# Token factors of the input norm moved behind the projections in a hybrid mLSTM and DeltaNet block, and x loaded in column slabs

## The chip, the cores and the metric

The kernel runs on one core of a Trainium2 chip. The metric is device time in microseconds (us), the median of three runs. A profile of one further execution is read beside it. Engines are named as the profile names them: PE is the matrix engine (PEld its weight loads), DVE the vector engine, ACT the scalar engine, POOL the GpSimd engine, SP the engine that only issues DMAs here. A "q" behind a name (SPq, ACTq) is the engine's sequencer, which issues DMAs.

## The reference

One decoder layer on x of 512 tokens by 2048 channels, all in float32. Cut to what matters here:

```python
def _rmsnorm(x, w=None):
    y = xf * lax.rsqrt(jnp.mean(xf * xf, axis=-1, keepdims=True) + NORM_EPS)
    return y if w is None else y * w.astype(jnp.float32)

u = _rmsnorm(h, norm_w)
proj = jnp.matmul(u, w_in.astype(jnp.float32))
(ml_q, ml_k, ml_v, ml_o, ml_z, ml_i, ml_f,
 dn_qkv, dn_z, dn_b, dn_a, gate_a, gate_b) = jnp.split(proj, idx, axis=-1)
h_a = _mlstm_chunkwise(q, k, v, i_pre, logf)               # 8 heads
h_a = _merge_heads(_rmsnorm(h_a)) * ml_norm_w * sigmoid(ml_o) * silu(ml_z)
qkv = _causal_conv_silu(dn_qkv, dn_conv_w)                 # along the tokens, width 4
h_b = _gated_delta_chunkwise(l2norm(dq), l2norm(dk), dv, beta, g)   # 16 heads
h_b = _merge_heads(_rmsnorm(h_b, dn_norm_w)) * silu(dn_z)
y = sigmoid(gate_a) * (h_a @ w_out[:2048]) + sigmoid(gate_b) * (h_b @ w_out[2048:])
return _rmsnorm(x + y, final_norm_w)
```

In the first line each token t has one factor, rsqrt(mean(x[t]^2) + eps). It multiplies the whole row of u, so it also multiplies every row of the projections, and it can be applied to them instead.

## The kernel before

Every matrix product is done in three passes with a high and a low part of each operand (`uh`, `ul` for u, `wh`, `wl` for weights). ACT makes the high part (a rounding copy, L140 for weights, L314 for u), DVE the low part (the difference, L143 and L315). PE's order is written out by hand, by the order of the code; the orders of the other engines are made by a scheduler from priorities (`urgent`, `behind`). Small pieces of work are generators that `tick()` advances, one tick per six matmuls.

The program has these stages:

- **Start.** SP issues x in eight pieces of 128 tokens by 1024 channels (L270), then the norm weights (L106) and the first four weight tiles `wr` (L172). For each of four groups of 128 tokens ACT squares and sums one half (L297), DVE the other (L299), DVE and POOL make the token factor `rs` (L301 to L304), and DVE and ACT scale the two halves of x in place (L290, L292). Then `make_u(kt)` turns one 128-channel block on PE (four transposes, L313) and ACT and DVE write `uh` and `ul` with the norm weight as a scale (L314, L315).
- **First projection**, `proj_cm(ML_Q)` with `first_block`: for each pair of channel blocks, PE transposes the blocks two ahead and then runs 12 matmuls (L257 to L259), so that u is made while it is used.
- **Three more projections, then `seven_stage`**: projections in blocks of 2 x 512 columns. Its ends are the functions `sink_z`, `sink_s`, `sink_q` and `sink_flat`, which bring the results out of PSUM through ACT and DVE.
- **Mixers** (from about 1110 to 1860 us): eight units of two DeltaNet heads, each with three projections (key, value, query), and eight mLSTM heads beside them. A projection leaves PSUM through `conv_in` (ACT's copy into `yp`, L828) and `conv_silu` (ACT's first tap, L835, and three multiply-adds of DVE, L837); `silu_end` adds the SiLU (ACT L843 into the tile `th`, DVE L844). `dn_back` inverts 128x128 triangles by blocks: among its steps DVE writes a small tile `s` (L1051), which PE needs at L1057.
- **Output projection** and final norm.

DMAs that SP and ACT issue tell of their landing by one of eight semaphores, given out in turn over both engines together (`DMAHW0` to `DMAHW7` in the listings below). A DMA that gets a semaphore for the second time waits until the DMA before it on that semaphore has landed, and the engine that issues it waits with it.

Of the kernel before, what the change touches and what calls it, by code (L numbers as in the profile page):

```python
# [8 lines left out]
F32 = mybir.dt.float32  # L9
# [6 lines left out]
P = 128  # L16
# [42 lines left out]
def hybrid_body(  # L59
# [24 lines left out]
    rows_d = dr.tile([32, S], F32, tag="rows", name="rows_d")  # L84
# [17 lines left out]
    bia = cp.tile([P, 96], F32, tag="bia", name="bia")  # L102

    def load_norms(tp, psp):
        nr = tp.tile([16, P], F32, tag="prow", name="nrow")
        nc.sync.dma_start(nr, norm_w.rearrange("(a p) -> a p", p=P))  # L106
# [20 lines left out]
    def turn_taps(crs, nr, psp):  # L127
        pt = psp.tile([P, 256], F32, tag="wk", name="pprt")
# [46 lines left out]
    def split_next():  # L175
        raw, nk, n = raws[len(parts)]
        with tc.high_priority(offset=2 * PRIO if len(parts) > SAHEAD else 0):
            hi = wp.tile([P, nk, n], F32R, tag="wh", name="wh", bufs=NSPL)
            lo = wp.tile([P, nk, n], F32R, tag="wl", name="wl", bufs=NSPL)
            with ExitStack() as first:  # L180
                if not parts:
                    first.enter_context(behind("V"))
                    first.enter_context(behind("A"))
                elif len(parts) == 1:
                    first.enter_context(tc.issue_after(done["V"]))
                    first.enter_context(tc.issue_after(done["A"]))
# [79 lines left out]
    xts = []  # L266
    for c in range(NC):
        xt = p0.tile([P, D], F32, tag=f"x{c}", name=f"xt{c}")
        for i in range(2):
            nc.sync.dma_start(xt[:, i * HD:(i + 1) * HD], x[c * P:(c + 1) * P, i * HD:(i + 1) * HD])  # L270
# [10 lines left out]
    rs = p0.tile([P, NC], F32, tag="rs", name="rs")  # L281
# [4 lines left out]
    sq, done = {}, {}  # L286

    def scale_x(c):
        with tc.issue_after(sq["V"]):
            newest["V"] = V.tensor_scalar(out=xts[c][:, 0:HD], in0=xts[c][:, 0:HD], scalar1=rs[:, c:c + 1], scalar2=None,  # L290
                                        op0=ALU.mult).ins
        newest["A"] = A.mul(xts[c][:, HD:D], xts[c][:, HD:D], rs[:, c:c + 1]).ins  # L292

    for c in range(NC):
        xt = xts[c]
        jk = p0.tile([P, HD], F32, tag="jk", name="jk", bufs=2)
        A.activation(jk, xt[:, 0:HD], AF.Square, accum_out=ss[:, c, 0:1])  # L297
        jv = p0.tile([P, HD], F32, tag="jv", name="jv", bufs=2)
        sq["V"] = V.scalar_tensor_tensor(out=jv, in0=xt[:, HD:D], scalar=1.0, in1=xt[:, HD:D], op0=ALU.mult, op1=ALU.mult,  # L299
# [5 lines left out]
        if c:  # L305
            scale_x(c - 1)
# [1478 lines left out]
```

## Time and profile before

| | us |
|---|---|
| median of 3 runs (2144.21 to 2146.49) | 2144.33 |
| profiled execution | 2143.23 |
| its span in the trace | 2141.5 |
| busy: PE / DVE / ACT / POOL | 2113.5 / 1708.0 / 1057.6 / 451.1 |

The span runs from the first to the last instruction of the trace; the execution's own time is 1.7 us longer. Busy times are sums over instructions. Matmuls overlap in the array, so a PE that is busy all the time can still differ in pace; the starts of its rows tell that.

### The profile page before, as it was taken

The page shows a single profiled execution, that of the slowest core. Times are in us where ns is not written, and L with a number is a line of the kernel's source. Part 1 is how long each engine was busy: PE and PEld are TensorE (multiplying, and loading weights), DVE is VectorE, ACT ScalarE, POOL GpSimd, SP SyncE. Part 2 cuts the span into 40 slices and gives each one's busy share as a digit, 9 for nine tenths or more (in the row PEclk, how much of TensorE's full clock was granted, in tenths as well). Part 3 has the DMA queues.
Part 4 walks back from the last instruction along what each step waited for, and adds up shares of the span by engine and source line. Part 5 has one row for each costly group of instructions (what it writes and reads, how often), then busy time and mean ns, then how long its engine had stood idle before and what let it go on. Part 6 is the DMA issues. An engine that isn't in the chain of part 4 may idle for free.

```text
span 2141.5 us, 32018 instructions
## 1 busy us (share of the span) xinstructions
PE 2113.5 (99%) x10544; PEld 1752.6 (82%) x10544; DVE 1708.0 (80%) x2981; ACT 1057.6 (49%) x2066; POOL 451.1 (21%) x667
## 2 busy tenths in 40 slices
PE   6999999999999999999999999999999999999998
PEld 5888888888888888888888888888888888887886
DVE  5888888788788778777766887888878878569887
ACT  5444454445444444444445546456465464345345
POOL 0000000000004000000003335344343363233211
PEclk9999999999999999999999999999999999999999
DMA  5355676667677767766766867777686677778895
GB/s 162 119 192 190 212 217 198 220 199 224 206 234 237 245 196 226 240 209 212 253 205 165 208 166 180 183 180 192 182 211 173 171 189 224 196 223 287 245 302 225
DMA packets 447144, 444.21 MB, mean 207 GB/s; under 512 B 197121, under 2 KB 303842, under 8 KB 446850
## 3 DMA queue, kind: packets, MB, share of 16 engines
q1 hardware_dynamic: 377618, 337.22, 53.9%
q0 software_dynamic: 24752, 72.90, 10.9%
q10 hardware_dynamic: 44608, 32.06, 4.8%
q8 instruction: 82, 1.34, 0.3%
q14 instruction: 84, 0.69, 0.1%
HBM read 348.66 MB, written 97.58 MB: 208 GB/s over the span
## 4 chain that ended last, share of the span: by engine, by line
PE 95%; DVE 2%; DMA 2%; issue 1%; SPq 0%; POOL 0%; ACT 0%; DVEq 0%; POOLq 0%; ACTq 0%
PE ps L578 18%; PE ps L580 18%; PE ps L579 18%; PE pj L257 10%; PE pj L259 9%; PE pj L258 9%; PE py L1407 2%; PE py L1409 2%; PE py L1408 2%; PE pk L915 1%; DMA wr<-in_w_out_dram 1%; PE pqk L990 1%; PE pw L1087 1%; PE pnum L1213 1%; PE po L1102 1%
## 5 line engine op out<-in xcount | busy, mean ns | idle before, releaser
L143 DVE TENSOR_TENSOR wl<-wr,wh 128x512 fp32r<-128x512 f32 (+1 forms) x522 | 444.3, 852 | 176.5 <-ACT wh L140 172.3
L140 ACT CAST wh<-wr 128x512 fp32r<-128x512 f32 (+1 forms) x522 | 373.9, 717 | 422.1 <-PE pj L258 218.5
L257 PE MATMUL pj<-uh,wh 128*128 128x512 f32 x896 | 375.8, 419 | 0.0
L259 PE MATMUL pj<-uh,wl 128*128 128x512 f32 x896 | 351.5, 392 | 0.0
L258 PE MATMUL pj<-ul,wh 128*128 128x512 f32 x896 | 349.8, 390 | 0.0
L578 PE MATMUL ps<-wh,uh 128*128 128x512 f32 x752 | 292.7, 389 | 0.8 <-DVE X L632 0.8
L579 PE MATMUL ps<-wl,uh 128*128 128x512 f32 x752 | 292.6, 389 | 0.0
L580 PE MATMUL ps<-wh,ul 128*128 128x512 f32 x752 | 292.6, 389 | 0.0
L140 ACT CAST wh<-t 128x1024 fp32r<-128x1024 f32 x120 | 126.3, 1053 | 301.7 <-PE ps L580 197.5
L533 POOL DMA_DIRECT2D t_d<-ts x104 | 56.6, 544 | 921.8 <-DVE ts L520 853.5
L579 PE MATMUL ps<-wl,suh 128*128 128x512 f32 x624 | 242.9, 389 | 0.0
L580 PE MATMUL ps<-wh,sul 128*128 128x512 f32 x624 | 242.8, 389 | 0.0
L578 PE MATMUL ps<-wh,suh 128*128 128x512 f32 x624 | 242.8, 389 | 0.0
L140 ACT CAST wh<-ts 128x512 fp32r<-128x512 f32 x240 | 147.9, 616 | 184.7 <-DVE ts L538 157.6
L143 DVE TENSOR_TENSOR wl<-t,wh 128x1024 fp32r<-128x1024 f32 x120 | 147.0, 1225 | 81.9 <-ACT wh L140 81.5
L259 PEld LDWEIGHTS pj<-uh,wl 128*128 128x128 f32 x896 | 168.3, 188 | 37.0
L257 PEld LDWEIGHTS pj<-uh,wh 128*128 128x128 f32 x896 | 169.2, 189 | 29.7
L258 PEld LDWEIGHTS pj<-ul,wh 128*128 128x128 f32 x896 | 169.3, 189 | 28.5
L143 DVE TENSOR_TENSOR wl<-ts,wh 128x512 fp32r<-128x512 f32 x240 | 164.9, 687 | 32.6 <-ACT wh L140 31.2
L578 PEld LDWEIGHTS ps<-wh,uh 128*128 128x128 f32 x752 | 141.2, 188 | 30.4 <-DVE X L632 1.2
L579 PEld LDWEIGHTS ps<-wl,uh 128*128 128x128 f32 x752 | 141.2, 188 | 29.5
L580 PEld LDWEIGHTS ps<-wh,ul 128*128 128x128 f32 x752 | 141.2, 188 | 29.2
(345 smaller groups left out, 3804.2 us busy)
## 6 DMA issues: line engine op xcount, KB each, us to landing
wr<-in_w_in_dram SPq DMA_DIRECT2D x744, 256.0 KB, 3.6
wr<-in_w_out_dram SPq DMA_DIRECT2D x138, 256.0 KB, 4.8
t_d<-ts POOLq DMA_DIRECT2D x104, 256.0 KB, 3.6
wr<-t_d SPq DMA_DIRECT2D x104, 256.0 KB, 3.7
xt<-in_x_dram SPq DMA_DIRECT2D x8, 512.0 KB, 7.2
tg_d<-X ACTq DMA_DIRECT2D x16, 256.0 KB, 4.8
tg_d<-to ACTq DMA_DIRECT2D x16, 256.0 KB, 4.6
v<-v_d SPq DMA_DIRECT2D x8, 512.0 KB, 5.6
```

The costliest lines, as they stand in the source:

```text
L140: newest["A"] = A.copy(hi, src).ins
L143: newest["V"] = V.tensor_tensor(out=lo, in0=src, in1=hi.bitcast(F32), op=ALU.subtract).ins
L257: T.matmul(ps[j], hi[:, k, wsl], uh[:, kt, :], start=(kt == 0), stop=False)
L258: T.matmul(ps[j], hi[:, k, wsl], ul[:, kt, :], start=False, stop=False)
L259: T.matmul(ps[j], lo[:, k, wsl], uh[:, kt, :], start=False, stop=(kt == KT - 1))
L533: queue.dma_start(t2_d[b % 2, i], ts[:, 0, :])
L578: T.matmul(ps[t], ah, hi, start=(g == "A" and i == 0), stop=False, skip_group_check=True)
L579: T.matmul(ps[t], ah, lo, start=False, stop=False, skip_group_check=True)
L580: T.matmul(ps[t], al, hi, start=False, stop=(i == KH - 1), skip_group_check=True)
L1407: T.matmul(ps[c], uh[:, kt, tsl], hi, start=(kt == ks[0]), stop=False)
L1408: T.matmul(ps[c], uh[:, kt, tsl], lo, start=False, stop=False)
L1409: T.matmul(ps[c], ul[:, kt, tsl], hi, start=False, stop=(kt == ks[-1]))
```

## The change

`rs` is no longer applied to x. The tiles of x go straight to the transposes, and they are loaded in column slabs: 256 channels of all tokens, 256 more, then three slabs of 512. Token groups 0 and 2 are issued by SP, 1 and 3 by ACT. The norm weights go through POOL's queue. The squares are taken during the first projection (`square_x`, one half group for each block from block 3 on), and `token_factors` makes `rs`, `rsh` (half of it) and `rsq` (with 1/sqrt(128)).

The factors come back in these places: in the scales of ACT's instructions in the sinks; in one multiplication of the gates; in the mLSTM heads' scores, weights and outputs and in the norms of the heads; and for the DeltaNet projections, which have tokens along the free axis, as a row `rsrow` broadcast to all partitions: `conv_in` becomes a multiplication on DVE. `th` in `silu_end` has one buffer in place of two.

```diff
     def load_norms(tp, psp):
-        nc.sync.dma_start(nr, norm_w.rearrange("(a p) -> a p", p=P))
+        nc.gpsimd.dma_start(nr, norm_w.rearrange("(a p) -> a p", p=P))
...
-    for c in range(NC):
-        xt = p0.tile([P, D], F32, tag=f"x{c}", name=f"xt{c}")
-        for i in range(2):
-            nc.sync.dma_start(xt[:, i * HD:(i + 1) * HD], x[c * P:(c + 1) * P, i * HD:(i + 1) * HD])
-        xts.append(xt)
-    for _ in range(2):
-        load_raw()
     load_norms(p0, psw)
+    xts = [p0.tile([P, D], F32, tag=f"x{c}", name=f"xt{c}") for c in range(NC)]
+
+    def load_x(a, b):
+        for c in range(NC):
+            (nc.scalar if c % 2 else nc.sync).dma_start(xts[c][:, a:b], x[c * P:(c + 1) * P, a:b])
+
+    load_x(0, NB)
+    load_raw()
+    load_x(NB, 2 * NB)
+    load_raw()
+    for a in range(2 * NB, D, NO):
+        load_x(a, a + NO)
...
-    def scale_x(c):
-        with tc.issue_after(sq["V"]):
-            newest["V"] = V.tensor_scalar(out=xts[c][:, 0:HD], in0=xts[c][:, 0:HD], scalar1=rs[:, c:c + 1], scalar2=None,
-                                        op0=ALU.mult).ins
-        newest["A"] = A.mul(xts[c][:, HD:D], xts[c][:, HD:D], rs[:, c:c + 1]).ins
...
+    def square_x(c, i):
+        xt, at = xts[c][:, i * HD:(i + 1) * HD], ss[:, c, i:i + 1]
+        jk = p0.tile([P, HD], F32, tag="jk", name="jk", bufs=2)
+        with tc.issue_after(done["V" if i else "A"]):
+            if i:
+                V.scalar_tensor_tensor(out=jk, in0=xt, scalar=1.0, in1=xt, op0=ALU.mult, op1=ALU.mult, accum_out=at)
+            else:
+                A.activation(jk, xt, AF.Square, accum_out=at)
+
+    def token_factors():
+        V.tensor_tensor(out=rs, in0=ss[:, :, 0], in1=ss[:, :, 1], op=ALU.add)
+        V.tensor_scalar(out=rs, in0=rs, scalar1=1.0 / D, scalar2=EPS, op0=ALU.mult, op1=ALU.add)
+        G.tensor_tensor(out=rs, in0=rs, in1=mhalf, op=ALU.pow)
+        V.tensor_scalar(out=rsh, in0=rs, scalar1=0.5, scalar2=None, op0=ALU.mult)
+        V.tensor_scalar(out=rsq, in0=rs, scalar1=float(P) ** -0.5, scalar2=None, op0=ALU.mult)
...
+        if 3 <= kt < 3 + 2 * NC:
+            square_x((kt - 3) // 2, (kt - 3) % 2)
+        if kt == 3 + 2 * NC:
+            token_factors()
...
                 with urgent(3):
-                    A.activation(o, ps, func, scale=scale)
+                    A.activation(o, ps, func, scale=scale[:, c:c + 1])
...
     def conv_in(ps, level=1):
...
         with urgent(level):
-            A.copy(yp[:, 3:S + 3], ps)
+            V.tensor_tensor(out=yp[:, 3:S + 3], in0=ps, in1=rsrow, op=ALU.mult)
...
-        th = wkb.tile([P, S], F32, tag="th", name="th", bufs=2)
+        th = wkb.tile([P, S], F32, tag="th", name="th", bufs=1)
...
         G.tensor_tensor(out=rsd, in0=ssq, in1=mhalf, op=ALU.pow)
+        G.tensor_tensor(out=rsd, in0=rsd, in1=rs, op=ALU.mult)
...
         with urgent():
-            V.tensor_tensor(out=w, in0=psc, in1=w, op=ALU.mult)
+            if first:
+                for c in range(NC):
+                    V.scalar_tensor_tensor(out=w[:, c, :], in0=psc[:, c, :], scalar=rs[:, c:c + 1], in1=w[:, c, :],
+                                           op0=ALU.mult, op1=ALU.mult)
+            else:
+                V.tensor_tensor(out=w, in0=psc, in1=w, op=ALU.mult)
```

PE's order of instructions is the same in both kernels, apart from one more small transpose and the turning of the parameters two blocks later. The other engines' orders move in three places that matter below.

The first place is ACT's start. The rows are ACT's first instructions in order, with the semaphores that each waits for (`DMAHW` the landings of DMAs, named after the engine otherwise). Before, ACT loads its table of functions at once and then squares x as it lands:

```order
L297 ACT_TABLE_LOAD
L297 ACTIVATE jk,ss<-xt_108 128x1024 [waits DMAHW0_49]
L297 ACTIVATE jk,ss<-xt_111 128x1024 [waits DMAHW2_49]
L292 ACTIVATE xt_108<-xt_108,rs 128x1024 [waits DMAHW1_49,Pool_49]
L297 ACTIVATE jk,ss<-xt_114 128x1024 [waits DMAHW4_49,Activation_49]
```

In the changed kernel the same engine stands so (`xt_114` and `xt_116` are token groups 1 and 3):

```order
L272 DMA xt_114<-in_x_dram 128x256
L272 DMA xt_116<-in_x_dram 128x256
L272 DMA xt_114<-in_x_dram 128x256
L272 DMA xt_116<-in_x_dram 128x256
L272 DMA xt_114<-in_x_dram 128x512 [waits DMAHW0_49]
L272 DMA xt_116<-in_x_dram 128x512 [waits DMAHW2_49]
L272 DMA xt_114<-in_x_dram 128x512 [waits DMAHW4_49]
L272 DMA xt_116<-in_x_dram 128x512 [waits DMAHW6_49]
L272 DMA xt_114<-in_x_dram 128x512 [waits DMAHW0_49]
L272 DMA xt_116<-in_x_dram 128x512 [waits DMAHW2_49]
L314 ACT_TABLE_LOAD [waits DVE_49]
L314 ACTIVATE uh<-put,normc 128x512 [waits PE_49] x2
```

Ten DMAs have moved ahead of ACT's table load and of its first work on u, and the last six of them wait for landings: `DMAHW0` and `DMAHW2` are waited for twice, the second time for the third slab.

The second place is the start of SP's order, before (`xt_108` to `xt_117` are the four token groups, two DMAs each):

```order
L270 DMA xt_108<-in_x_dram 128x1024 x2
L270 DMA xt_111<-in_x_dram 128x1024 x2
L270 DMA xt_114<-in_x_dram 128x1024 x2
L270 DMA xt_117<-in_x_dram 128x1024 x2
L106 DMA nrow<-in_norm_w_dram 16x128 [waits DMAHW0_49]
L172 DMA wr<-in_w_in_dram 128x2x256 [waits DMAHW1_49]
```

and in the changed kernel (`xt_113` and `xt_115` are token groups 0 and 2):

```order
L272 DMA xt_113<-in_x_dram 128x256
L272 DMA xt_115<-in_x_dram 128x256
L272 DMA xt_113<-in_x_dram 128x256
L176 DMA wr<-in_w_in_dram 128x2x256
L272 DMA xt_115<-in_x_dram 128x256 [waits DMAHW1_49]
L272 DMA xt_113<-in_x_dram 128x512 [waits DMAHW3_49]
L176 DMA wr<-in_w_in_dram 128x2x256 [waits DMAHW5_49]
L272 DMA xt_115<-in_x_dram 128x512 [waits DMAHW7_49]
```

The first weights moved from the tenth place to the fourth, and the last piece of the second slab (the second `xt_115`) waits for the landing of the very first piece.

The third place is DVE's queue where the value projection of a unit leaves PSUM, in the middle of the mixers. Before:

```order
L143 TENSOR_TENSOR wl<-wr,wh 128x512 x2
L1251 TENSOR_TENSOR mg<-v_12723,mg 128x512
L1051 TENSOR_TENSOR s_13367<-p_13358,cs 64x256
L860 STREAM_TRANSPOSE to<-mg 128x512
L837 SCALAR_TENSOR_TENSOR vt<-yp_9793,convc,vt 128x512
```

In the changed kernel, the same place:

```order
L147 TENSOR_TENSOR wl<-wr,wh 128x512 x2
L1267 TENSOR_TENSOR mg<-v_12751,mg 128x512
L834 TENSOR_TENSOR yp_9802<-pj,rsrow 128x512
L1057 TENSOR_TENSOR s_13398<-p_13389,cs 64x256
L866 STREAM_TRANSPOSE to<-mg 128x512
L834 TENSOR_TENSOR yp_9804<-pj,rsrow 128x512
L147 TENSOR_TENSOR wl<-wr,wh 128x512
L843 SCALAR_TENSOR_TENSOR vt<-yp_9802,convc,vt 128x512
```

The new multiplication of `conv_in` stands ahead of `s`, on which PE waits. It stands there in five of the eight units; in the first two it comes behind `s`, and in the last one `s` comes later than all projections.

More of the change, by code (lines that the diff above doesn't have):

```diff
@@ L83, in hybrid_body @@
     dr = ctx.enter_context(tc.tile_pool(name="dr", bufs=1, space=DRAM))
-    rows_d = dr.tile([32, S], F32, tag="rows", name="rows_d")
+    rows_d = dr.tile([33, S], F32, tag="rows", name="rows_d")
     h_d = dr.tile([KT, 16, BS, 4, BS], F32, tag="hd", name="h_d")
@@ L125, in load_params, with turn_taps @@
         return crs, nr
-    def turn_taps(crs, nr, psp):
-        pt = psp.tile([P, 256], F32, tag="wk", name="pprt")
+    def turn_taps(crs, nr, psp, rr):
+        pt = psp.tile([P, 384], F32, tag="wk", name="pprt")
+        T.transpose(pt[0:NC, 256:384], rs, ident)
+        V.tensor_copy(rr, pt[0:NC, 256:384])
+        nc.sync.dma_start(rows_d[32, :].rearrange("(c t) -> c t", t=P), rr)
         T.transpose(pt[:, 192:209], nr, ident[0:17, 0:17])
@@ L180, in split_next @@
             with ExitStack() as first:
[L181 to L184, printed above, removed]
+                if len(parts) == 1:
                     first.enter_context(tc.issue_after(done["V"]))
```

53 lines of the change are left out of this document (23 added, 30 removed).

## Prediction

> **What bounds the kernel now.** I read the page of the profile first (busy times, then the chain that ended last), then the busy times by stage, then the order of time of the first 25 us. The page:
>
> ```profile
> PE 2113.5 (99%) x10544; PEld 1752.6 (82%) x10544; DVE 1708.0 (80%) x2981; ACT 1057.6 (49%) x2066; POOL 451.1 (21%) x667
> ...
> PE 95%; DVE 2%; DMA 2%; issue 1%; SPq 0%; POOL 0%; ACT 0%; DVEq 0%; POOLq 0%; ACTq 0%
> ```
>
> PE is the bound: 95% of the chain is its work. The busy times by stage (stretch, its length, then PE, PEld, DVE, ACT, POOL with counts, then the granted clock and DMA) show where it is not:
>
> ```profile
> 0.00:21.00 21.00, 4.33 (x18) 3.63 (x19) 10.86 (x25) 12.90 (x19) 3.26 (x14) 1.00 0.87 274
> 21.00:60.00 39.00, 39.00 (x198) 31.08 (x197) 19.60 (x34) 17.61 (x31) 0.61 (x2) 1.00 0.33 95
> 100.00:1080.00 980.00, 980.00 (x4332) 811.22 (x4331) 797.84 (x1022) 455.03 (x652) 77.31 (x136) 1.00 0.68 217
> 1130.00:1800.00 670.00, 669.70 (x4011) 560.54 (x4010) 551.22 (x1376) 378.19 (x1020) 271.94 (x370) 1.00 0.73 184
> ```
>
> From 21 us on PE never rests for long. So time can be won only in the first 21 us, and lost wherever another engine makes PE wait. The change does both: it shortens the start, and it adds work to DVE in the mixers (the last row, DVE busy 551 of 670 us).
>
> The start, in order of time (start, length, engine, line, what, count; in brackets the idle time before and its releaser):
>
> ```profile
> 0.73 1.28 ACT L297 ACT_TABLE_LOAD   x1 [0.73 <-PEq L1772]
> 0.74 3.85 SPq L270 DMA_DIRECT2D xt<-in_x_dram  x8
> 4.60 1.06 ACT L297 ACTIVATE jk<-xt 128x1024 f32<-128x1024 f32 x1 [2.58 <-DMA xt<-in_x_dram]
> ...
> 17.21 1.15 ACT L292 ACTIVATE xt<-xt,rs 128x1024 f32<-128x1024 f32 x1 [1.48 <-POOL rs L304]
> 18.02 3.04 PE L313 MATMUL put<-ident,xt 128*128 128x128 f32 x13 [1.28 <-DVE xt L290]
> 20.70 0.78 PE L257 MATMUL pj<-uh,wh 128*128 128x512 f32 x1
> 21.28 0.63 PE L258 MATMUL pj<-ul,wh 128*128 128x512 f32 x1
> 21.70 0.58 PE L259 MATMUL pj<-uh,wl 128*128 128x512 f32 x1
> 22.12 0.39 PE L257 MATMUL pj<-uh,wh 128*128 128x512 f32 x1
> 22.35 0.40 PE L258 MATMUL pj<-ul,wh 128*128 128x512 f32 x1
> ```
>
> The chain is: all of x lands, the last group is squared and scaled (17.21), PE transposes (18.02), and the first projection starts at 20.70. Its matmuls start every 0.42 us up to 22.12, and every 0.23 us after that.
>
> **The start, step by step.** The new kernel needs only the first slab to transpose, so the squares, the factor and the scaling leave this chain. What comes late next? From the order of the code, ACT does: it issues ten DMAs, six of them behind landings, before its table load and the first `uh`. That an issue really waits for a landing is seen in SP's rows of before, where the weights wait in this way:
>
> ```profile
> 5.79 0.40 SPq L172 DMA_DIRECT2D wr<-in_w_in_dram  x1
> 8.01 0.37 SPq L172 DMA_DIRECT2D wr<-in_w_in_dram  x1
> 9.31 0.37 SPq L172 DMA_DIRECT2D wr<-in_w_in_dram  x1
> ```
>
> These are the moments when the second, third and fourth 512 KB piece of x had landed; with ACT's first square at 4.60 (the first piece) they are also the landing curve: 0.5 MB by 4.6, 1 MB by 5.8, 1.5 MB by 8.0, 2 MB by 9.3. I take the new transfers by the same curve. Eight issues took 3.85 us on SP, 0.48 each; two queues issue their first four by 2.6 us, 1.15 MB together. ACT's fifth and sixth issue wait for its first two pieces (about 4.1 and 4.6, the first 0.5 MB). Its last issue waits until the sixth has landed. Ahead of that stand the 1.15 MB, the last piece of the second slab (0.13), two pieces of the third on ACT's queue (0.5) and one on SP's (0.25): 2.0 MB. By the curve that is 9.3; by 0.5 MB each 1.25 us from 4.6, without the gap between 5.8 and 8.0, it is 8.3. I take 8.7. Then come one issue (0.45), the table load (1.28), two `uh` and one `wh`:
>
> ```profile
> L314 ACT ACTIVATE uh<-put,normc 128x512 fp32r<-128x512 f32 x14 | 9.1, 686 | 0.6 <-PE put L313 0.4
> L140 ACT CAST wh<-wr 128x512 fp32r<-128x512 f32 x10 | 6.0, 617 | 10.4 <-PE pj L258 7.2 <-DMA wr<-in_w_in_dram 3.1
> ```
>
> 8.7 + 0.45 + 1.28 + 1.3 + 0.6 = 12.3 us for the first matmul, **8.4 us earlier** than 20.70. The bounds: without ACT's waits only the second slab would count (1.4 MB, about 7.5) and eight transposes at 0.23 us (13 in 3.04), 9.3 us; if the curve runs a third slower, 15 us. The norm weights, now on POOL's queue, are hidden: even before, 8 KB had 4 us of cover on this chain.
>
> The first matmuls run slow, and more of them than before. From 18.02 PE worked without a break and changed pace at 22.12, 4.1 us later. In the new kernel the 16 transposes are over by about 9.5, PE stands still until 12.3, and I let the 4.1 us begin anew: about ten slow matmuls instead of four, six times 0.2 us, **1.2 us lost** (bounds 0 and 3).
>
> The Trainium skill, page "TensorE: Matmul & The Clock Gate", Part 1 (The HAM clock gate) says that the array runs at half its clock until it has been busy for about 3.4 us, and again after an idle window as long; its Part 4 (PE-mode transpose) says that transposes do not count as busy. The rows of before speak against the second: the pace changed 1.4 us after the first matmul, so the transposes had counted. By that page the eight slow matmuls would begin at the first one in either kernel, and the sum would lose 0.8 us instead of 1.2.
>
> The squares now run beside PE. A pair of blocks costs PE 12 matmuls and 8 transposes, about 3.6 us. DVE then has two `ul`, one `wl` and one square for it:
>
> ```profile
> L315 DVE SCALAR_TENSOR_TENSOR ul<-put,normc,uh 128x512 fp32r<-128x512 f32 x14 | 10.0, 746 | 0.5 <-ACT uh L314 0.2
> L299 DVE SCALAR_TENSOR_TENSOR jv<-xt 128x1024 f32<-128x1024 f32 x4 | 4.9, 1226 | 8.3 <-DMA xt<-in_x_dram 8.3
> ```
>
> 1.5 + 0.7 + 1.3 is 3.5, ACT has less, and u is made two blocks ahead: I cost this at nothing. Without that cover each of the four pairs would lose the 1.2 us of a square, 5 us.
>
> **The mixers.** ACT's 48 copies go, and 48 multiplications come to DVE. The nearest rows are ACT's copy and a DVE product of the same size out of PSUM:
>
> ```profile
> L828 ACT COPY yp<-pj 128x512 f32<-128x512 f32 x48 | 28.0, 583 | 21.4 <-PE pj L259 21.3
> L917 DVE TENSOR_TENSOR aq<-pk,dm 128x512 f32<-128x512 f32 x16 | 11.1, 691 | 7.3 <-PE pk L915 5.6 <-ACT dm L898 1.1 <-ACT gb L903 0.3
> ```
>
> 48 x 0.69 = 33 us, beside 119 us in which DVE stands idle there (670 - 551). On the average that fits, so what counts are the places where PE stands close behind DVE. The place in the third listing is one. The rows of before, in the third unit:
>
> ```profile
> 1413.27 1.57 DVE L143 TENSOR_TENSOR wl<-wr,wh 128x512 fp32r<-128x512 f32 x1 [2.91 <-ACT wh L140]
> ...
> 1413.66 0.59 ACT L828 COPY yp<-pj 128x512 f32<-128x512 f32 x1
> ...
> 1414.76 0.68 DVE L1251 TENSOR_TENSOR mg<-v,mg 128x512 f32<-128x512 f32 x1
> 1415.47 0.41 DVE L1051 TENSOR_TENSOR s<-p,cs 64x256 f32<-64x256 f32 x1
> ...
> 1416.15 0.27 PE L1056 MATMUL p<-tb,s 64*64 64x64 f32 x1
> 1416.16 0.27 PE L1057 MATMUL p<-s,ta 64*64 64x64 f32 x1
> ...
> 1416.77 0.50 PE L257 MATMUL pj<-uh,wh 128*128 128x512 f32 x1
> ```
>
> `s` ends at 1415.88 and PE uses it at 1416.16. A multiplication of 0.69 ahead of it moves its end to about 1416.5, so PE waits **0.4 us, in five units 2.0 us**. Behind the multiplication also stand the next `wl` and the convolution's own steps, which PE needs some microseconds later. The last unit's chain (the norm, the gate, a transpose, DMAs out and in) ends in waits of PE:
>
> ```profile
> PE ps L578 <- DVE X L632: 0.8, 1, 0.8
> PE ps L578 <- DVE X L1431: 0.7, 2, 0.5
> ```
>
> It gets one more multiplication on POOL and a busier DVE; I add 0.7 us (bounds 0 and 2). For the smaller edits (the split of the scores in four heads, a column instead of a number as ACT's scale, the eight late scalings of v on ACT, the one buffer of `th`, the gates' factor) I add 0.5 us; ACT's spare half covers most, and without it they could cost 3 us.
>
> **The sum:** 8.4 - 1.2 - 2.0 - 0.7 - 0.5 = 4.0 us won. The profiled execution took 2143.23 us (a span of 2141.5 and 1.7 around it), so 2139.2; the median stands 1.1 higher, which gives **2140.3 us**.
>
> **The rivals.** About 0.2% (4.3 us) is what a measurement of this kernel can tell from no change; the line to "faster" lies at 2140.0, next to my sum.
>
> - *Nothing is given back in the mixers.* DVE's idle time takes all, as its average says; the waits of 0.4 us vanish if DVE comes earlier to that place. 8.4 - 1.2 = 7.2: 2137.1.
> - *ACT is not held at the start* (pieces land earlier, or its waits are over when they come). First matmul at 9.3, 11.4 won, less 1.2 and 3.2: 2137.3; without losses in the mixers 2134. For it: the queue moved 0.5 MB in 1.25 us in steady flow. Against it: ten issues and a table load stand in order ahead of the first `uh`.
> - *The start gives little*: first matmul at 15, more slow matmuls or late weights; 5.7 - 2 - 3.2 leaves 0.5: 2143.8.
> - *Slower: PE waits for PSUM at each projection.* Three buffers serve two tiles per projection, so the next projection's second tile needs the first one freed. In the rows above ACT's copy starts at 1413.66, and PE writes that buffer again at 1416.77, 3.1 us later; DVE's queue there (two `wl`, `mg`, to 1415.44) takes 1.8 of that and the product 0.7. If DVE runs 2 us later than now at these points, each of 24 projections waits 1.4 us: 34 us, about 2171. Waits begin from 0.6 us of added lag, and the kernel is slower from 0.5 us of wait at each projection (7.2 + 4.3 = 11.5 us in all). For it: DVE is busy 82% there and rises to 87%. Against it: PE's whole wait for DVE in that stretch is now one of 0.3 us:
>
> ```profile
> PE pw L1087 <- DVE r L1082: 0.3, 1, 0.3
> ```
>
> - *The change doesn't do what it says*: the transposes could still wait for all of x. The order speaks against it, since the first ones wait for four landings only; it has no chance of its own.
>
> **How the numbers follow.** Forecast (2138 to 2143) 0.48, of which 0.22 below 2140.0; nothing given back 0.18, of which 0.16 below; ACT not held 0.12, all below; the start gives little 0.12; slower 0.10. So faster 0.50, same 0.40, slower 0.10. The range 2134.5 to 2146 leaves out the slow case and the far ends of the others, about 0.17.
>
> **What would show it.** In the new trace: ACT's table load behind its DMA issues, at 9 to 10 us, not at 0.7; the first matmul at 12.3, and the pace of 0.23 us some 4 us later; no idle time of PE up to 50 us; at the value projections of the later units 0.4 us of PE waiting for `s`. I am wrong if the table load stands near 5, if PE waits in the first projection, or if PE's waits for DVE in the mixers sum to over 5 us.

## The result, and the profile after

| | before | after |
|---|---|---|
| median (range), us | 2144.27 (2143.45 to 2146.49, 4 runs) | 2156.58 (2156.07 to 2157.85, 4 runs) |
| span of the profiled execution, us | 2141.5 | 2154.3 |

The ratio is 1.0057, 95% interval 1.0039 to 1.0074: **the change costs 12.3 us**. The prediction was 2140.3 with a range to 2146, so it had the wrong sign. The two lines of the page that answer to those of before, busy time and chain:

```profile
PE 2119.7 (98%) x10545; PEld 1754.5 (81%) x10545; DVE 1735.1 (81%) x3035; ACT 1043.4 (48%) x2022; POOL 453.5 (21%) x690
...
PE 69%; issue 12%; DVE 8%; DMA 5%; ACT 3%; POOL 1%; SPq 1%; ACTq 0%; DVEq 0%; POOLq 0%
```

PE's share of the chain fell from 95% to 69%; DVE's rose from 2% to 8%. Where that is, the stretches show (PE, PEld, DVE, ACT, POOL):

```profile
0.00:21.00 21.00, 11.31 (x46) 8.94 (x47) 4.86 (x8) 6.84 (x11) 1.84 (x11) 1.00 0.92 281
21.00:60.00 39.00, 38.63 (x195) 30.64 (x193) 26.00 (x58) 19.84 (x38) 1.65 (x3) 1.00 0.36 102
100.00:1080.00 980.00, 979.53 (x4321) 810.87 (x4320) 797.46 (x1020) 466.14 (x654) 78.97 (x145) 1.00 0.67 217
1130.00:1800.00 670.00, 661.76 (x3953) 551.17 (x3952) 573.13 (x1412) 350.15 (x959) 267.16 (x382) 1.00 0.72 180
```

In the first 21 us PE now works 11.3 us (4.3 before). The start in the order of time:

```profile
0.74 9.86 ACTq L272 DMA_DIRECT2D xt<-in_x_dram  x10
...
8.38 1.54 PE L313 MATMUL put<-ident,xt 128*128 128x128 f32 x6 [0.84 <-DMA xt<-in_x_dram]
10.69 1.28 ACT L314 ACT_TABLE_LOAD   x1 [10.69 <-DMA xt<-in_x_dram]
...
13.81 0.79 PE L258 MATMUL pj<-uh,wh 128*128 128x512 f32 x1 [3.88 <-ACT wh L144]
...
16.64 0.60 PE L258 MATMUL pj<-uh,wh 128*128 128x512 f32 x1
17.07 0.42 PE L259 MATMUL pj<-ul,wh 128*128 128x512 f32 x1
17.33 0.39 PE L260 MATMUL pj<-uh,wl 128*128 128x512 f32 x1
```

As forecast, ACT's ten DMA issues hold its table load, and PE waits 3.9 us behind the transposes; the matmuls come every 0.43 us up to 17.07. In the mixers (the stretch from 1130 us) it stands idle 8.2 us, where it was 0.3. PE executes the same matmuls in the same order in both kernels, apart from the one small transpose, so the starts of matching matmuls can be subtracted (after less before):

| place | after less before, us |
|---|---|
| first matmul (20.70 before, 13.81 after) | -6.9 |
| behind the slow matmuls | -5.9 |
| at 44 us | -5.3 |
| at 523 us (one wait for `wl`) | -4.7 |
| at 1781 us, all units but the last | +6.3 |
| at 1843 us, in the last unit | +11.1 |
| end | +12.8 |

The start won 4.7 us net, the mixers lost 11.0, the last unit 4.8 more, the output stage 1.7. Of the last unit's 4.8 about 3.0 are one wait for `wl`. Behind that wait the granted clock (the third number from the end of this row) is 0.50 for 3.4 us, and matmuls that start every 0.23 us elsewhere start every 0.43 us. That costs 1.6 more:

```profile
1839.81:1843.22 3.41, 3.41 (x38) 2.75 (x38) 1.66 (x3) 0.75 (x2) 2.96 (x5) 0.50 0.70 214
```

The waits of PE from 1130 us to the end (what waited, on what, sum, times, longest):

```profile
PE p L1063 <- DVE s L1057: 5.3, 4, 1.7
PE py L1424 <- DVE wl L147: 2.8, 1, 2.8
PE pw L1093 <- DVE r L1088: 1.5, 2, 0.8
PE ps L584 <- DVE wl L147: 1.1, 1, 1.1
...
PE pj L258 <- DVE yp L834: 0.3, 1, 0.3
```

The first row is the place that the prediction named: PE waits for `s` at the value projection. It forecast 0.4 us in five units. In the order of time the place costs 0.35, 0.34, 0.90, 1.20, 1.73 and 1.99 us in six units, 6.5 in all: the price grows from unit to unit. (In the first of the six the multiplication stands behind `s`.) The rest of the mixers' 11.0 lies around the first unit (1.7), at the first matmul of a projection in three units (1.6) and at 1781 us (1.0). DVE and PE at the place of `s`, in the fourth unit, and PE in two later ones:

```profile
1498.16 0.69 DVE L147 TENSOR_TENSOR wl<-wr,wh 128x512 fp32r<-128x512 f32 x1 [2.91 <-ACT wh L144]
1498.78 1.53 DVE L1267 TENSOR_TENSOR mg<-v,mg 128x512 f32<-128x512 f32 x1
1500.34 0.69 DVE L834 TENSOR_TENSOR yp<-pj,rsrow 128x512 f32<-128x512 f32 x1
1500.94 0.41 DVE L1057 TENSOR_TENSOR s<-p,cs 64x256 f32<-64x256 f32 x1
...
1501.40 0.27 PE L1063 MATMUL p<-s,ta 64*64 64x64 f32 x1 [0.77 <-DVE s L1057]
...
1677.14 0.27 PE L1063 MATMUL p<-s,ta 64*64 64x64 f32 x1 [1.60 <-DVE s L1057]
...
1764.94 0.27 PE L1063 MATMUL p<-s,ta 64*64 64x64 f32 x1 [1.70 <-DVE s L1057]
```

A multiplication of 0.69 ahead of `s` can't make a wait of 1.7. DVE must already be late when it gets there. Its 2.91 us of idle time just ahead don't make up for that. It waits there for ACT's `wh`, and ACT has itself stood waiting for a tile `ta` of DVE, longer than in the kernel before (after, then before; 4.14 us in the seventh unit after):

```profile
1493.15 0.74 ACT L1048 COPY tb<-p 32x256 f32<-32x256 f32 x2 [3.55 <-DVE ta L1044]
```

```profile
1494.10 0.73 ACT L1042 COPY tb<-p 32x256 f32<-32x256 f32 x2 [2.83 <-DVE ta L1038]
```

Upstream, some 30 us earlier in the unit, POOL shows a second thing that the prediction had passed over. Here `rsd` is the norm's factor of a head, `gz` the head's gate, which `rsd` scales, and `xi` a tile of the triangles' inversion, cleared for the next round. POOL's rows after:

```profile
1461.01 1.00 POOL L1127 TENSOR_TENSOR rsd<-ssq,mhalf 128x4 f32<-128x4 f32 x1
...
1462.64 1.31 POOL L1001 TENSOR_TENSOR kq<-kq,gb 128x512 f32<-128x512 f32 x1
1463.90 0.21 POOL L1128 TENSOR_TENSOR rsd<-rsd,bia 128x4 f32<-128x4 f32 x1
1467.20 0.32 POOL L961 MEMSET xi<- 128x256 f32 x1 [3.09 <-DMA xd<-xi]
...
1468.60 1.05 POOL L1129 TENSOR_TENSOR gz<-gz,rsd 128x512 f32<-128x512 f32 x1
...
1469.69 0.69 DVE L1132 TENSOR_TENSOR gz<-po,gz 128x512 f32<-128x512 f32 x1 [4.69 <-POOL gz L1129]
```

and the same place before:

```profile
1465.15 1.31 POOL L995 TENSOR_TENSOR kq<-kq,gb 128x512 f32<-128x512 f32 x1
1466.40 1.05 POOL L1122 TENSOR_TENSOR gz<-gz,rsd 128x512 f32<-128x512 f32 x1
1467.38 0.32 POOL L955 MEMSET xi<- 128x256 f32 x1
```

The new multiplication of `rsd` (L1128) takes 0.2 us. But it made a chain of two POOL instructions out of one, and the scheduler now sets the clearing of `xi` ahead of `gz`. That clearing waits for a DMA out of `xi`, 3.1 us, `gz` waits behind it, and DVE stands idle 4.7 us for `gz`, in each of four units (4.69, 4.44, 4.49 and 4.20).

### The profile page after: what moved, and what is told of

It is laid out like the page before. It is cut to its first block, busy times and chain, and to the rows that moved or that the text cites. A ratio compares the mean times of both kernels' runs of the same rounds, so it can differ in the third digit from the quotient of the medians.

```text
span 2154.3 us, 32062 instructions
## 1 busy us (share of the span) xinstructions
PE 2119.7 (98%) x10545; PEld 1754.5 (81%) x10545; DVE 1735.1 (81%) x3035; ACT 1043.4 (48%) x2022; POOL 453.5 (21%) x690
## 4 chain that ended last, share of the span: by engine, by line
PE 69%; issue 12%; DVE 8%; DMA 5%; ACT 3%; POOL 1%; SPq 1%; ACTq 0%; DVEq 0%; POOLq 0%
PE ps L584 14%; PE ps L585 14%; PE ps L583 14%; PE pj L258 6%; PE pj L260 6%; PE pj L259 6%; DVE wl L147 2%; PE py L1423 1%; PE py L1424 1%; PE py L1425 1%; ACT wh L144 1%; DVE kq L843 1%; DVE xi L972 1%; DVE tmp L970 1%; ACT njk L860 1%
## 5 line engine op out<-in xcount | busy, mean ns | idle before, releaser
L147 DVE TENSOR_TENSOR wl<-wr,wh 128x512 fp32r<-128x512 f32 (+1 forms) x522 | 436.6, 837 | 162.1 <-ACT wh L144 158.2
```

The costliest lines, as they stand in the source:

```text
L147: newest["V"] = V.tensor_tensor(out=lo, in0=src, in1=hi.bitcast(F32), op=ALU.subtract).ins
```

## The experiments

So two theories stood: **A**, the 48 multiplications of `conv_in` fill DVE; **B**, POOL's new instruction makes DVE late. The results of all runs, each as a ratio to the kernel before in runs on the same chip:

| run | median us | ratio (95% interval) |
|---|---|---|
| after | 2156.6 | 1.0057 (1.0039 to 1.0074) |
| conv on ACT | 2147.5 | 1.0012 (1.0004 to 1.0021) |
| rsd on DVE | 2151.9 | 1.0029 (1.0018 to 1.0040) |
| both | 2144.3 | 0.9993 (0.9984 to 1.0001) |
| both, two `th` | 2143.9 | 0.9996 (0.9987 to 1.0005) |
| value conv on ACT | 2143.4 | 0.9992 (0.9983 to 1.0001) |
| DVE load | 2146.8 | 1.0007 (0.9998 to 1.0016) |
| conv on POOL | 2179.0 | 1.0159 (1.0139 to 1.0179) |
| before + rsd | 2187.6 | 1.0196 (1.0182 to 1.0210) |
| before + rsd, no new tile | 2149.5 | 1.0016 (1.0007 to 1.0025) |
| before + 16 bytes | 2186.4 | 1.0187 (1.0173 to 1.0201) |
| start only | 2141.3 | 0.9980 (0.9971 to 0.9988) |
| start, x on SP | 2142.7 | 0.9986 (0.9977 to 0.9995) |
| start, weights early | 2142.0 | 0.9980 (0.9971 to 0.9989) |
| start, gates' weights on POOL | 2136.8 | 0.9963 (0.9950 to 0.9975) |
| whole 2 | 2179.0 | 1.0155 (1.0137 to 1.0174) |
| whole 3 | 2145.8 | 1.0006 (0.9996 to 1.0016) |
| whole 4 | 2144.9 | 1.0000 (0.9991 to 1.0009) |
| whole 5 | 2150.7 | 1.0027 (1.0017 to 1.0038) |

A step of 0.0010 is 2.1 us; differences between runs below are differences of these ratios. By the intervals such a difference is uncertain by about 3 us, and by about 4 where the changed kernel is one of the two.

**Conv on ACT.** One line of the changed kernel:

```diff
-            V.tensor_tensor(out=yp[:, 3:S + 3], in0=ps, in1=rsrow, op=ALU.mult)
+            A.copy(yp[:, 3:S + 3], ps)
```

> The changed kernel with the 48 evictions of conv_in back on ACT as plain copies; the token factor of the DeltaNet projections is left out. Theory A (the 48 multiplications fill DVE behind each projection, and PE's waits for s, for r and for wl come from that): those waits go, the 18 us lost between 44 us and the end come back almost whole, and the time is the start's gain alone, about 2139 to 2141. Theory B (POOL's new multiplication of rsd pushes the second head's gz behind the clearing of xi, DVE waits 4.5 us for it and runs late from there): that wait stays, PE still waits for s more from unit to unit, and the time falls by at most half of the 18, to 2147 or more.

It gave back 9.6 us (1.0057 to 1.0012). PE's waits for `s` stayed, 3.5 us in all. Theory A alone would have given 2139 to 2141. The time and the waits that stayed fit B's forecast, but the fall is about as large as B allowed, so `conv_in` is a large part of the loss and not the whole.

**Rsd on DVE.**

```diff
-        G.tensor_tensor(out=rsd, in0=rsd, in1=rs, op=ALU.mult)
+        with urgent(): V.tensor_tensor(out=rsd, in0=rsd, in1=rs, op=ALU.mult)
```

> The changed kernel with one instruction moved: the multiplication of rsd by rs goes from POOL to DVE (128x4, two in each unit); PE's order is the same. Theory A: DVE has the same work and 0.3 us more per unit; 2156 to 2158. Theory B: gz comes before xi again, DVE's idle time ahead of the second gz falls from 4.5 us to below 1, and PE's wait for s no longer grows from unit to unit (0.4 us each as forecast instead of 0.35 to 2.0); 2148 to 2152.

6.0 us came back, within theory B's forecast. POOL has `gz` ahead of `xi` again, and DVE's wait for it is 0.94:

```profile
1467.20 1.42 POOL L1129 TENSOR_TENSOR gz<-gz,rsd 128x512 f32<-128x512 f32 x1 [0.60 <-DVE rsd L1128]
1469.75 0.32 POOL L961 MEMSET xi<- 128x256 f32 x1 [1.13 <-DMA xd<-xi]
...
1468.66 0.69 DVE L1132 TENSOR_TENSOR gz<-po,gz 128x512 f32<-128x512 f32 x1 [0.94 <-POOL gz L1129]
```

The wait of 2.8 us for `wl` in the last unit went with it, though PE now waits 1.7 us for another tile, `tn`, there. PE's waits for `s` are still 4.4 us, and not 0.4 in each unit as B forecast. They no longer grow steadily. In "conv on ACT" they didn't either, so the steady growth needs both causes. One of the waits, of 1.7 us at 1677 us, is followed by 3.4 us at a granted clock of 0.50, which costs 1.5 us more in the profiled execution.

**Both**, the two edits together:

> The changed kernel with both edits of the first two runs together: conv_in on ACT as a plain copy (the token factor of the DeltaNet projections is left out) and the multiplication of rsd by rs on DVE. The two alone gave 9 and 5 us. If the two causes are separate and together carry the mixers' loss: 2141 to 2143, the time of the start alone (2141.3), and PE's waits for s below 1 us in all. If they are one cause seen twice (either cure should then have been enough by itself to bring back most): 2146 to 2147.

0.9993, 13.7 us below the changed kernel. The edits alone gave 9.6 and 6.0, so they are two causes and nearly add up. PE no longer waits for `s`. The time is 1.3 us above the forecast for two separate causes.

**Both, two `th`.** The one buffer of `th` made two again:

> The kernel that took 2144.3 us (conv_in a plain copy on ACT, rsd's factor on DVE; the token factor of the DeltaNet projections is left out) with two buffers of th in place of one and the then unused row gone. If the one buffer of th holds the SiLU's ends and with them DVE (PE's five waits at pqk of 0.3 us each): those waits go, 2141 to 2142. If the 3 us over the start-only kernel come from the split scores, v1, we and the norms: 2144 to 2145.

No difference (0.9996). The 2.8 us between "both" and "start only" are among the split scores, `we`, `v1`, the norms of the heads and the place of `rsd`; they were not separated further. In the traces of both runs PE loses 0.6 us in each of five units at one place (`pqk`, where it waits for DVE's `aq`), and in "start only" nothing there: 3.0 together. What makes `aq` late stays open.

**Value conv on ACT.** On top of "rsd on DVE", ACT copies at the value projections alone:

```diff
-            V.tensor_tensor(out=yp[:, 3:S + 3], in0=ps, in1=rsrow, op=ALU.mult)
+            A.copy(yp[:, 3:S + 3], ps) if ct >= 32 else V.tensor_tensor(out=yp[:, 3:S + 3], in0=ps, in1=rsrow, op=ALU.mult)
```

> The changed kernel with rsd's factor on DVE (2151.9 us), and the value projections alone, 16 of the 48 evictions, back on ACT as plain copies (their token factor is left out). If the cost of conv_in sits at the value projection, ahead of s, as the prediction had it: PE's waits for s (4.4 us) go, and 5 us or more of the 7.6 come back, 2145 to 2147. If every projection costs alike, by DVE's load: a third comes back, 2149 to 2150.

0.9992: 7.9 us came back, as much as with all three projections on ACT (7.7). The 32 multiplications at the key and the query projections cost nothing that can be measured; the 16 at the value projections cost it all. (Of the 7.9, the profiled execution of "rsd on DVE" had 1.5 in its stretch at half the clock.) The 16 us behind `s` in the fourth unit fit that, in DVE's column (before, "rsd on DVE", and this run):

```profile
1501.70:1517.70 16.00, 16.00 (x95) 13.40 (x94) 13.60 (x34) 5.50 (x12) 8.33 (x7) 1.00 0.95 244
```

```profile
1502.90:1518.90 16.00, 15.99 (x92) 13.63 (x93) 14.81 (x35) 6.34 (x13) 4.29 (x7) 1.00 0.94 244
```

```profile
1500.60:1516.60 16.00, 16.00 (x95) 13.34 (x94) 12.93 (x31) 5.72 (x12) 8.27 (x7) 1.00 0.93 241
```

DVE is busy 85% of this stretch before, 93% with the multiplications, and 81% in this run: this is where it has little to spare.

**DVE load.** On top of "both", an operation of the same size that nothing waits for:

```diff
             A.copy(yp[:, 3:S + 3], ps)
+            V.tensor_tensor(out=rsrow, in0=yp[:, 3:S + 3], in1=rsrow, op=ALU.min)
```

> As the kernel that took 2144.3 us (conv_in a plain copy on ACT, rsd's factor on DVE; the token factor of the DeltaNet projections is left out), but DVE does 48 operations of 128x512 beside it, one for each conv_in with the same priority, whose results nothing waits for. If DVE's load is what costs (it fills the stretches behind a projection, whatever the operation is for): 2150 to 2153, as with the real multiplication (2151.9). If the place of the multiplication in the chain from PSUM to the first tap is what costs: 2144 to 2146.

1.0007: 3.0 us of the 7.7, with intervals of 2 us on either side. Load alone doesn't seem to carry it: in the 16 us behind `s` of the fourth unit DVE is as busy here (14.80) as in "rsd on DVE" (14.81). In this kernel the operation stands behind `s`, and ACT's first tap needn't wait for it; DVE's own taps still stand behind it in the queue.

**Conv on POOL.** On top of "rsd on DVE":

```diff
-            V.tensor_tensor(out=yp[:, 3:S + 3], in0=ps, in1=rsrow, op=ALU.mult)
+            A.copy(yp[:, 3:S + 3], ps)
+            G.tensor_tensor(out=yp[:, 3:S + 3], in0=yp[:, 3:S + 3], in1=rsrow, op=ALU.mult)
```

> The changed kernel, whole, with rsd's factor on DVE, and conv_in as ACT's copy followed by a multiplication by the row on POOL, in place (128x512, 48 of them, about 1.1 us each by POOL's products of that size). PSUM is freed as early as before and DVE does what it did before. Theory (DVE's load of 33 us is what conv_in costs, 2151.9 against 2144.3 with the plain copy): 2145 to 2148, the rest being POOL's later answers and its slowing of DVE. Rival (the convolution's chain as a whole is what PE waits for, so that each us added ahead of the first tap counts): 2155 or more, as POOL's 1.1 us stand in that chain and DVE's 0.7 did.

2179: the rival's "2155 or more" holds, the theory doesn't. The view of the groups gives POOL's multiplication 1164 ns, and the list of waits has 15.2 us for `s`:

```profile
L835 POOL TENSOR_TENSOR yp<-yp,rsrow 128x512 f32<-128x512 f32 x48 | 55.5, 1164 | 18.7 <-ACT yp L834 13.8 <-DVE xi L973 3.3 <-DVE wm L1207 1.1
...
PE p L1064 <- DVE s L1058: 15.2, 6, 3.4
```

**Before + rsd.** The POOL part of the change alone, put into the kernel before:

```diff
+    ones = cp.tile([P, NC], F32, tag="ones", name="ones"); G.memset(ones, 1.0)
...
         G.tensor_tensor(out=rsd, in0=ssq, in1=mhalf, op=ALU.pow)
+        G.tensor_tensor(out=rsd, in0=rsd, in1=ones, op=ALU.mult)
```

> The kernel before with one small POOL instruction added behind each rsd (times a tile of ones), nothing else changed: the POOL part of the change alone. Theory A: 2144, no change. Theory B: the order on POOL turns as in the changed kernel, DVE waits for gz, but has 4 us per unit less to do than in the changed kernel, so PE loses 0 to 1 us per unit: 2144 to 2150.

42 us slower, which no theory had. PE hardly waits (1.6 us in all); nearly every matmul takes longer, from the start on. Only the tile `ones`, 16 bytes per partition, could reach back to the start. Two runs tell the tile from the instruction.

**Before + rsd, no new tile** (the ones in spare columns of `bia`):

> The kernel before with the same small POOL instruction behind each rsd as in the earlier run that took 2187.6 us, but the ones stand in four spare columns of bia, so that no other tile's place in SBUF moves. In the earlier run every 128x512 matmul came 0.006 us later (its mean 395 ns against 389), from the start on, and PE hardly waited. If the 16 bytes per partition of the added tile slowed the matmuls: 2144 to 2150 here, with 389 ns. If the POOL instruction did: 2187 again.

**Before + 16 bytes** (the tile alone, written once):

```diff
+    pad = cp.tile([P, NC], F32, tag="pad", name="pad"); G.memset(pad, 1.0)
```

> The kernel before with a tile of 16 bytes per partition added that nothing reads (set once by POOL at the start). If the shift of the tiles behind it by 16 bytes slows the matmuls: about 2186, with 395 ns per matmul. If not: 2144.

The instruction costs 3.4 us (1.5 to 5.4) even in the kernel before, which confirms B without any part of A. The tile costs 40 us. In the same 980 us PE gets through 4223 recorded matmuls instead of 4332, 232 ns each instead of 226 (a group of matmuls before, then the same group, another one and the stretch with the 16 bytes):

```profile
L579 PE MATMUL ps<-wl,suh 128*128 128x512 f32 x621 | 241.7, 389 | 0.0
```

```profile
L579 PE MATMUL ps<-wl,suh 128*128 128x512 f32 x592 | 233.9, 395 | 0.0
...
L579 PE MATMUL ps<-wl,s4h 128*128 128x512 f32 x192 | 74.6, 389 | 0.0
...
100.00:1080.00 980.00, 980.00 (x4223) 789.88 (x4223) 780.06 (x1003) 444.30 (x635) 75.13 (x132) 1.00 0.67 212
```

The group with `s4h` as its other operand keeps its 389 ns, though its weights are `wl` too, so not every matmul is slowed. The changed kernel has 4321 in that stretch, so it isn't touched by this: it keeps its factors in spare columns of `bia`.

**Start only**: all edits of the mixers undone.

> The changed kernel with all edits of the mixers undone (conv_in on ACT, no factor in rsd, sm, the scores, we and v1, two buffers of th); the token factor is left out in the mixers, the start, the sinks and the gates stay as changed. If the start's gain, which was 5.4 us in the new trace at 44 us, is carried to the end: 2139. If the sinks and the gates in the first half cost something, or the gain is lost at a later wait that does not depend on the edits of the mixers: 2141 to 2144.

0.9980, 4.3 us faster than before. The start's gain is real and most of it reaches the end; the forecast of 2139 was for all of it.

**Start, x on SP**, on top of that:

```diff
-            (nc.scalar if c % 2 else nc.sync).dma_start(xts[c][:, a:b], x[c * P:(c + 1) * P, a:b])
+            (nc.scalar if c % 2 and b <= 2 * NB else nc.sync).dma_start(xts[c][:, a:b], x[c * P:(c + 1) * P, a:b])
```

> The start-only kernel (2141.3 us; the token factor is left out in the mixers) with the third to fifth slabs of x issued by SP alone, so that ACT issues four DMAs that wait for nothing in place of ten of which six wait. If ACT's issues held the first uh, as the prediction said: the table load stands at 2.5 to 3 us in place of 10.7, the first matmul comes at 9 to 10.5 in place of 13.5, and the time is 2137 to 2138.5. If the landing of the second slab or of the first weights holds it all the same: first matmul at 12 or later, 2140 to 2141.

The mechanism was right and the time was not. The table load stands at 5.32, behind the norm weights `normc`, and not at 2.5 to 3. In the order of time:

```profile
5.32 1.28 ACT L314 ACT_TABLE_LOAD   x1 [5.32 <-DVE normc L110]
...
8.44 0.80 PE L258 MATMUL pj<-uh,wh 128*128 128x512 f32 x1
...
9.74 0.39 PE L258 MATMUL pj<-uh,wh 128*128 128x512 f32 x1
9.97 0.40 PE L259 MATMUL pj<-ul,wh 128*128 128x512 f32 x1
...
19.11 0.52 PE L258 MATMUL pj<-uh,wh 128*128 128x512 f32 x1 [2.46 <-ACT wh L144]
```

The first matmul comes 5.2 us earlier than in "start only", and all of that is lost by 26 us: at 19.11 PE has waited 2.5 us for the third weight tile, which SP issued behind eleven pieces of x. Behind this wait the granted clock is 0.50 for 6.8 us, and the slow matmuls there cost the rest:

```profile
19.46:26.28 6.82, 5.74 (x16) 4.07 (x15) 4.39 (x7) 2.09 (x4) 0.00 (x0) 0.50 0.40 63
```

**Start, weights early**: `load_raw()` ahead of each of the three later slabs.

> The start-only kernel (2141.3 us; the token factor is left out in the mixers) with the later slabs of x on SP alone, as in the run that took 2142.7 us, and in addition one weight tile issued ahead of each of the three later slabs. In that run the first matmul came at 8.44, 5.2 us earlier than in the start-only kernel, but PE stood idle 2.5 us at 19.1 for the third weight tile, which SP had issued behind eleven pieces of x, and the matmuls behind the idle time were slow again until all 5.2 us were lost. If the place of the weights in SP's queue did that: no idle time of PE over 1 us before 30 us, and 2136 to 2138. If the DMA engines as a whole are too slow for x and the weights together: idle time shifts to another tile and the time stays at 2140 to 2143.

Again nothing: the next late input was the gates' weights `wgp`, and the wait for them is again followed by half the granted clock (0.50 from 27.27 to 30.67).

```profile
27.44 0.74 PE L324 MATMUL pgr<-uh,wgp 128*112 128x512 f32 x1 [3.62 <-DVE wgp L147]
```

**Start, gates' weights on POOL**: `nc.gpsimd.dma_start` for the two DMAs of `wg`.

> The start-only kernel (token factor left out in the mixers) with the later slabs of x on SP, a weight tile ahead of each of them, and now the two DMAs of the gates' weights on POOL's queue. In the run without this last edit (2142.0) the first matmul came at 8.8, but PE stood idle 3.6 us at 27.4 for the gates' weights, and slow matmuls followed. If that was the last late input: no idle time over 1 us up to 50 us, and about 2137 (5 us less than the start-only kernel's 2141.3, less what waits of 1 to 1.5 us later on take). If another input is late next, or the gates' small pieces hold up x: 2140 to 2143.

0.9963, 8.0 us faster than before, and no wait of PE over 1 us from the first matmul (11.02) up to 50 us. Three late inputs stood one behind another (ACT's `uh`, the third weight tile, the gates' weights), and the time only moved when all three were gone.

**Whole kernels, nothing left out.** Whole 2 has the POOL multiplications and the better start but for the gates' weights; whole 3 is "rsd on DVE" with the best start; whole 4 adds that at the value projections ACT copies and DVE multiplies in place behind `s`; whole 5 has POOL do these 16.

> The changed kernel, whole, with three edits together: rsd's factor on DVE, conv_in as ACT's copy and POOL's multiplication, and the start with the later slabs on SP and one weight tile ahead of each. If the start's earlier first matmul (8.4 in place of 13.8) is kept by the weights' new place and POOL carries conv_in: 2140 to 2143, under the kernel before. If either fails: 2145 to 2155.

> The whole changed kernel, nothing left out, with rsd's factor on DVE and the new start (later slabs on SP, a weight tile ahead of each, the gates' weights on POOL's queue). rsd's factor gave 5 us (2151.9). If the start gives 4 to 5 more: 2147 to 2148, still slower than before by 2 to 3, as conv_in's 7 us stay. If the start gives nothing: 2152.

> The whole kernel that took 2145.8 us (rsd's factor on DVE, the new start), with one more edit: at the value projections ACT copies PSUM out and DVE then multiplies in place, so that DVE's 48 multiplications are all still there but s now stands ahead of them in all units. If the place ahead of s is what costs: 2138 to 2141, faster than both kernels, and PE's waits for s below 1 us. If the load of the 16 multiplications costs, wherever they stand: 2144 to 2146.

> As the other kernel of this pair, but the 16 multiplications of the value projections on POOL, behind ACT's copy, and s ahead of whatever follows. If the place ahead of s is what costs and DVE's load does not: about as the other kernel. If POOL's longer operation delays the first taps and POOL's other answers, as with all 48 on POOL (2179): 2145 to 2155.

Whole 2 failed as "conv on POOL" had, whole 3 came out a little under its forecast, and whole 5 as forecast for POOL's longer operation. The best is whole 4, 1.0000: the same as before. Against whole 3 it gained 1.3 us, less than the intervals, so "the place ahead of `s` is what costs" failed as forecast. PE's waits for `s` fell from 5.2 to 2.8 us, not below 1, and one of them, 1.7 us at 1671 us, is followed by 3.4 us at a granted clock of 0.50. But the same edit puts ACT's copy into the chain from PSUM to the taps, so what the place costs by itself is not shown. The multiplications stand in that chain and in a stretch where DVE has little time left, and the bare load gave 3 us; how much is place, chain and load stays open. No whole version beat the kernel before.

## Why the prediction was wrong, point by point

- **The start, 8.4 won less 1.2.** Mostly right. ACT was held by its DMA issues: the table load stood at 10.69, behind a landing of x, and "start, x on SP" moved it to 5.3 and the first matmul to 8.44. The landing curve was 1.5 us too fast, so the first matmul came at 13.81 instead of 12.3. The slow matmuls, eight and not ten, cost 1.0 instead of 1.2. "I cost this at nothing", said of the squares beside the first projection, was right: from 17.5 to 38 us the difference stays at -5.9. What had no term is the small transpose of `rs`. PE waits for DVE's copy of it (`rr`), and the place costs 0.6:

```profile
43.39 0.23 PE L133 MATMUL pprt<-ident,nrow 17*128 17x17 f32 x1 [0.37 <-DVE rr L131]
```

  One wait for `wl` at 523 us takes 0.6 more. Such a wait, of up to 1.7 us, stands at about 520 and at about 2010 us in the kernels with the new start; its cause was not looked into.
- **The value projections, 2.0 lost.** Right place, wrong price: 7.9 us by the run that undoes them alone. The step that failed is "On the average that fits, so what counts are the places where PE stands close behind DVE", with the delay then counted once per unit. DVE's idle time was not a reserve that could be drawn on anywhere: 2.9 us of it, in six of the eight units, is one wait for ACT (the 2.91 in the row of 1498.16), which had waited for DVE, and the stretch behind the value projection was 85% busy already. A delay there was not made up before the next unit. The prediction's own sign of being wrong, waits of PE for DVE of over 5 us, showed: 5.3 for `s` alone.
- **The edits costed within 0.7 and 0.5.** "One more multiplication on POOL" stood among the 0.7 us of the last unit, and had no term for the units before it. It costs 6.0 with `conv_in` on DVE (and 4.1 with it on ACT, from "conv on ACT" to "both"), by an order that turned: the clearing of `xi`, which waits for a DMA, went ahead of `gz`. The step that failed is the reading of the order: the places shown were ACT's, SP's and DVE's, and POOL's turn, which an order shows, was not among them. `th` costs nothing that can be measured; the rest of the small edits costs 2.8, uncertain by about as much.
- **The last unit, 0.7 lost.** It lost 4.8: 3.0 at the wait for `wl`, which went with `rsd` on DVE, and 1.6 in the 3.4 us at half the granted clock behind it. The prediction had slow matmuls only at the start, and no price for what follows a wait.
- **The rival on the slower side** had the right sign and the wrong mechanism: waits for PSUM at each projection. PE waited for `yp` once, 0.3 us, and the delays at the first matmul of a projection are 1.6 of the 11.0. That DVE's queue turns a delay into waits elsewhere was not among the rivals.
- **ACT's scale as a column** costs 0.1 us each, hidden as said. Two groups of one sink, before and after:

```profile
L685 ACT ACTIVATE to<-X 128x512 f32<-128x512 f32 x8 | 5.0, 622 | 0.0
```

```profile
L689 ACT ACTIVATE to<-X,bia 128x512 f32<-128x512 f32 x8 | 5.7, 718 | 0.0
```

  The Trainium skill, page "ScalarE: Activation LUTs", What ACT_TABLE_LOAD costs, says that each pointer operand adds about 93 ns; the rows agree (96).

## What to carry to other kernels

An engine's average idle time is no budget: ask in which stretch it lies and whether it is a wait in a chain, and price added work at the busiest stretch. Read the new order of every engine, the nearly idle ones too: a 0.2 us instruction can turn an order and let a wait for a DMA stand ahead of work that others need. When one late input is cured, name the next one before counting the gain. A wait of PE can cost more than its length: look at the granted clock behind it.

## What the runs showed of the hardware

- **16 bytes of SBUF cost 1.9%.** A tile of 16 bytes per partition that nothing reads made most 128x512 matmuls 6 ns slower (226 to 232), 40 us in all; the group with `wl` and `s4h` kept its pace (389 ns each). That it acts by moving the tiles behind it is argued: the traces show no addresses. Which operand it is, and which addresses are good, was not tried. The Trainium skill, page "SBUF — State Buffer", Operand start alignment, gives the rule for legal addresses and says that it is no statement on speed.
- **POOL's work slows DVE's.** The `mg` product takes 0.68 us alone, and beside a POOL product 1.53 us in the changed kernel (at 1498.78) and 1.57 in the one before (at 1328.30). The Trainium skill, page "GPSIMD Engine Reference", Key points, says that the two share their SBUF interfaces when DVE reads two inputs there; this agrees.
- **Transposes count for the pace of the matmuls.** In "start, x on SP" the matmuls behind sixteen transposes run at 0.23 us from 9.74 on, 1.3 us after the first; in the changed kernel, with 3.9 us of idle time between, it takes 3.3 us (13.81 to 17.07). The Trainium skill, page "TensorE: Matmul & The Clock Gate", Part 4 (PE-mode transpose), says that PE-mode transposes don't count as busy in the same way; the rows speak against it, as those of before did. The granted clock of the first 21 us reads 1.00 in the changed kernel all the same, but that is no reading: the trace's first record of the clock is at 17.09 us (22.09 before the change), where the pace changes, and the view takes what lies ahead of it as full.
- **Behind some waits of PE its clock is halved.** Behind waits of 1.7 us ("rsd on DVE", whole 4), 2.5 ("start, x on SP"), 2.8 (the changed kernel) and 3.6 ("start, weights early") the granted clock reads 0.50 for 3.4 us, in the second case for 6.8. Behind the waits of 1.60 and 1.70 us for `s` in the changed kernel it doesn't. What decides was not tried.
